# A decoder trunk's attention heads: last products, output copy and split emitted later, inside the next head's turn

## The chip, the cores and the metric

The kernel runs on one core of a Trainium2 chip. The metric is the device time in microseconds of one execution; lower is better. Times given are medians of several executions.

## The reference

The program is a decoder trunk of two layers on one sequence of 512 tokens and 1024 features, in float32: a gated linear attention layer with its convolutional feed-forward part, then keys and values computed once from the residual stream, then a sparse attention layer (NSA) with a second feed-forward part, and a final normalisation. The change touches the sparse attention alone. Cut to that:

```python
p_cmp = masked_softmax(q @ k_cmp * scale, cmp_end <= pos)     # compressed branch, 31 blocks
o_cmp = p_cmp @ v_cmp
p_sel = masked_softmax(rope(q) @ k_sel * scale, kpos <= qpos) # selected blocks
o_sel = p_sel @ v_sel
p_win = masked_softmax(rope(q) @ k_win * scale, win_mask)     # sliding window of 512
o_win = p_win @ v_win
o = gates[0] * o_cmp + gates[1] * o_sel + gates[2] * o_win
x = x + o @ w_o
```

There are 16 heads of 64 features in 4 groups that share keys and values. With 512 tokens, 8 blocks of 64 and up to 16 selected, all blocks are selected and the window covers all of the past, so both branches are causal attention over the whole sequence, each with its own keys and values.

## The kernel before, in words

Activations lie feature by token (`xT`, eight tiles of 128 x 512). To keep float32 accuracy, every large product is made of three passes of a reduced format: each operand is split into a rounded part `h` (ScalarE, ACT) and a remainder `l` (VectorE, DVE, or GpSimd, POOL), and `mm3` (L235 to L239) multiplies hh, lh and hl on TensorE (PE).

The attention stage is `nsa_att`. For one head, two generators emit its instructions piece by piece:

- `scores(h)` (L866) makes the softmax of a head in six score groups over the four blocks `i` of 128 queries and the two branches `b`. A group multiplies queries and keys (L882, L883), adds the causal mask by a product with an identity (L884), takes the row maximum on DVE (L886), and the exponential on ACT with the row sum beside it (L893). The result goes to `p_t`, one of ten buffers; the score bank `sc` has three. After half the groups a reciprocal (L902) and the gates (L903) give the scale of each row, and the rows are scaled by DVE (L913), by ACT (L909) or in pieces of 128 columns by POOL (L911, in `pool_parts`, L151), as the string `SCALE_ENGINE` says: POOL has block 0 of branch 0 and block 3 of branch 1.
- `values(h)` (L921) transposes the probabilities in five packs (L939, bank `tp`, two buffers), copies a pack to SBUF on ACT (L941, `pt_h`), subtracts on DVE (L943, `pt_l`), and two packs later multiplies by the values (`products`, L931, bank `po`, one buffer). The last two packs' products follow after the fifth pack (L948, L949), then two products for the compressed branch (L952). The output is evacuated by an ACT copy of its lower half (`lo`, L957) and a DVE addition (`o_t`, L958); after every second head `o_t` is split (L960).

The heads' loop (L984) interleaves the scores of head h+1 with the values of head h by the string `INTERLEAVE`:

```python
INTERLEAVE = "ssvsvsvsvs"
```

After it comes the rest of `values(h)` (L996), then the rest of the scores. Once in four heads the compressed branch of the next group runs: `compressed` (L836) makes its scores (L842, bank `pC`) and softmax, whose subtraction of the maximum is on POOL (L849) and whose exponential on ACT (L850); `compressed_t` (L858) transposes it. Between heads the loop emits `queries(f)` (rotary embedding by `rope`, L677, in POOL pieces `rot` and `sw`, then the split `q_s`) and, at a lower priority, a `query()` (a projection `pl` of 24 products, whose weights `w_raw` are copied by ACT, L159, and split by POOL, `w_l`) or a part of the output projection.

The code's order sets priorities only. A scheduler in the framework takes, engine by engine, the ready instruction of the highest priority and fixes the program's order; on the chip each engine then works through its own list in order and waits on semaphores.

Of the kernel before, what the change touches and what calls it, by code (L numbers as in the profile page):

```python
# [79 lines left out]
def tile_kernel(ctx: ExitStack, tc: tile.TileContext, a, out):  # L80
# [20 lines left out]
    def T(shape, dt, name):  # L101
        tag = TAGS.get(name, name)
        pool, n = home[tag]
        return pool.tile(shape, dt, name=name, tag=tag, bufs=n)

    def P(name):
        return T([128, 512], F32, name)
# [59 lines left out]
    def split(src, name, eng=DVE):  # L167
        h = T([128, S], F32R, name + "_h")
        ACT.activation(h, src, AF.Copy)  # L169
        l = T([128, S], F32R, name + "_l")  # L170
        eng.tensor_tensor(l, src, h, OP.subtract)  # L171
        return h, l
# [68 lines left out]
    def proj(src, xs, name, w=None, pool=False, m=128):  # L241
        n = len(xs)
        h, l = w or load_w(src, [128, n, m], pool=pool)
        ps = P(name)
        for k in range(n):
            mm3(ps[0:m], (h[:, k], l[:, k]), xs[k], k == 0, k == n - 1)
        return ps
# [407 lines left out]
    def nsa():  # L655
        with pools("nsa"):
            with pools("p_att"):
                os_ = nsa_att()
            with pools("p_proj"):
                for d in range(KT):  # L660
                    wo_part(os_, 4, d)

    def wo_part(os_, k0, d):
        add_x(d, proj(a["nsa_o"][d][:, k0:k0 + 4], os_[k0:k0 + 4], "pw", pool=k0 == 0))

    def nsa_att():
# [38 lines left out]
        def query():  # L705
            ps = proj(a["nsa_q"][len(Q)], xq, "pl" if len(Q) > 1 else "sc", pool=len(Q) > 1)
            q = T([128, S], F32, "qn")
            DVE.scalar_tensor_tensor(q, ps, 0.125, rb, OP.mult, OP.mult)
            Q.append(q)
# [3 lines left out]
        def queries(f):  # L713

            t = rope(Q[f])
            r = []
            for x in range(2):
                for hh in range(2):
                    n, o = slice(hh * 64, hh * 64 + 64), slice(64 - hh * 64, 128 - hh * 64)
                    y = T([128, S], F32R, "q_s")  # L720
                    if x == 0:
                        ACT.activation(y[n], t[n], AF.Copy)
                    else:
                        pool_parts(y[n], t[n], r[hh][n], OP.subtract)
                    nc.sync.dma_start(y[o].bitcast(F32), y[n].bitcast(F32))
                    r.append(y)
            for hh in range(2):
                QS[2 * f + hh] = (r[hh], r[2 + hh])
# [107 lines left out]
        def compressed(g):  # L836
            pC = P("pC")
            pCv = pC.rearrange("p (t c) -> p t c", t=4)
            for f in range(2):
                q = Q[2 * g + f]  # L840
                for i in range(4):
                    PE.matmul(pCv[:, i, f * 64:(f + 1) * 64], q[:, i * 128:(i + 1) * 128], BD[:, g],  # L842
                              start=True, stop=True)
            pc = CP[g] = T([128, 4, 4, 32], F32, "pcm")
            DVE.tensor_tensor(pc, pC.rearrange("p (t h n) -> p t h n", t=4, h=4),
                              cmask[:, :, None, :].to_broadcast([128, 4, 4, 32]), OP.add)
            mx = small([128, 4, 4], "mx", bufs=2)
            DVE.tensor_reduce(mx, pc, AX.X, OP.max)
            POOL.tensor_tensor(pc, pc, mx[:, :, :, None].to_broadcast([128, 4, 4, 32]), OP.subtract)  # L849
            ACT.activation(pc, pc, AF.Exp)  # L850
            sm = small([128, 4, 4], "smc", bufs=2)
            DVE.tensor_reduce(sm, pc, AX.X, OP.add)
            DVE.reciprocal(sm, sm)
            DVE.tensor_tensor(sm, sm, gate[:, :, 0, g * 4:g * 4 + 4], OP.mult)
            DVE.tensor_scalar(sm[:, 0], sm[:, 0], rowmask, None, OP.mult)
            POOL.tensor_tensor(pc, pc, sm[:, :, :, None].to_broadcast([128, 4, 4, 32]), OP.mult)

        def compressed_t(g):  # L858
            pT = P("pT")
            for i in range(4):  # L860
                PE.transpose(pT[:, i * 128:(i + 1) * 128], CP[g][:, i].rearrange("p a b -> p (a b)"), ident)
            CP[g] = split(pT, "pc")
# [58 lines left out]
        def values(h):  # L921
            g, gi = divmod(h, 4)
            pr = PR.pop(h)
            o_ps = P("po")
            todo = []

            def products():
                pack, th, tl = todo.pop(0)
                for b, j, c0 in pack:
                    for t in (th, tl):  # L930
                        PE.matmul(o_ps[:, j * 128:], V[b][:, j, g], t[:, c0:c0 + (4 - j) * 128],  # L931
                                  start=(b, j) == (0, 0) and t is th, stop=False)

            for pack in packs:
                tp = P("tp" if h < 15 or pack[0][1] % 2 else "sc")
                for b, j, c0 in pack:
                    for i in range(j, 4):
                        c = c0 + (i - j) * 128
                        PE.transpose(tp[:, c:c + 128], pr[i, b][:, j * 128:(j + 1) * 128], ident)  # L939
                th = T([128, S], F32R, "pt_h")  # L940
                ACT.activation(th, tp, AF.Copy)  # L941
                tl = T([128, S], F32R, "pt_l")
                DVE.tensor_tensor(tl, tp, th, OP.subtract)  # L943
                todo.append((pack, th, tl))
                if len(todo) > 2:
                    products()
                yield
            while todo:  # L948
                products()  # L949
            qd = slice(gi * 32, (gi + 1) * 32)  # L950
            for x in range(2):
                PE.matmul(o_ps, Vc[qd, g], CP[g][x][qd], start=False, stop=x == 1)  # L952
            hs = slice((gi % 2) * 64, (gi % 2) * 64 + 64)
            if gi % 2 == 0:
                half[0] = T([128, S], F32, "o_t")
            lo = T([128, S], F32, "lo")
            ACT.activation(lo[hs], o_ps[64:128], AF.Copy)  # L957
            DVE.tensor_tensor(half[0][hs], o_ps[0:64], lo[hs], OP.add)  # L958
            if gi % 2:
                os_.append(split(half[0], "o"))  # L960
            yield

        def run(g, n=99):
            for _ in range(n):
                if next(g, 1):
                    return
# [14 lines left out]
        queries(1)  # L981
        compressed(0)
        query()
        for h in range(16):  # L984
            gs = scores(h + 1) if h + 1 < 16 else None
            if h % 4 == 2 and h < 14:
                compressed(h // 4 + 1)
            gv = values(h)
            for n, c in enumerate(INTERLEAVE):
                if h == 0 and n == 6:  # L990
                    compressed_t(0)
                if c == "v":
                    run(gv, 1)
                elif gs:
                    run(gs, 1)
            run(gv)  # L996
            if gs:
                run(gs)
            if h % 4 == 3 and h < 14:
                compressed_t(h // 4 + 1)  # L1000
            if h % 2 == 1 and h // 2 + 2 < 8:
                queries(h // 2 + 2)
            if h in QUERY_HEAD:
                with tc.high_priority(offset=-50):
                    query()
            for d in range(KT):
                if WO_HEAD[d] == h:
                    with tc.high_priority(offset=-50):
                        wo_part(os_, 0, d)
# [102 lines left out]
```

## Time and profile before

| | us |
|---|---|
| median of 3 runs | 1331.68 |
| lowest and highest | 1331.22, 1332.91 |
| the profiled execution's own time | 1331.54 |
| span of its instructions | 1329.7 |
| busy: PE, DVE, ACT, POOL | 1312.2, 896.3, 610.8, 180.6 |

The span runs from the first instruction to the last; 1.8 us lie around it. Busy time is the time in which an engine had an instruction in work. Matmuls overlap, and their ends are modelled, so the time from one matmul's start to the next one's start tells more than busy time does. PE's granted clock is a share of 2.4 GHz. The attention heads run from about 730 to 935 us of the span.

### The profile page before, as it was taken

The page shows a single profiled execution, that of the slowest core. Times are in us where ns is not written, and L with a number is a line of the kernel's source. Part 1 is how long each engine was busy: PE and PEld are TensorE (multiplying, and loading weights), DVE is VectorE, ACT ScalarE, POOL GpSimd, SP SyncE. Part 2 cuts the span into 40 slices and gives each one's busy share as a digit, 9 for nine tenths or more (in the row PEclk, how much of TensorE's full clock was granted, in tenths as well). Part 3 has the DMA queues.
Part 4 walks back from the last instruction along what each step waited for, and adds up shares of the span by engine and source line. Part 5 has one row for each costly group of instructions (what it writes and reads, how often), then busy time and mean ns, then how long its engine had stood idle before and what let it go on. Part 6 is the DMA issues. An engine that isn't in the chain of part 4 may idle for free.

```text
span 1329.7 us, 17541 instructions
## 1 busy us (share of the span) xinstructions
PE 1312.2 (99%) x6498; PEld 1079.2 (81%) x6498; DVE 896.3 (67%) x1427; ACT 610.8 (46%) x1030; POOL 180.6 (14%) x454
## 2 busy tenths in 40 slices
PE   9999999999999999999999899999999999999998
PEld 6899988888888888888887677777888888888886
DVE  6888665577636763676765798888777736763672
ACT  6434544344314431443254687786554413441342
POOL 2000000000000000000236756653000000000000
PEclk9999999999999999999999899999999999999999
DMA  6122213333332333325543211211433332332331
GB/s 203 61 64 64 64 48 96 95 95 95 96 95 95 96 96 94 97 81 166 152 128 88 64 41 36 60 41 32 128 95 95 95 95 96 96 96 94 97 109 64
DMA packets 42246, 119.89 MB, mean 90 GB/s; under 512 B 5488, under 2 KB 8432, under 8 KB 42160
## 3 DMA queue, kind: packets, MB, share of 16 engines
q1 hardware_dynamic: 41152, 117.15, 29.0%
q10 hardware_dynamic: 1008, 1.61, 0.3%
q8 instruction: 51, 0.84, 0.3%
q14 instruction: 35, 0.29, 0.1%
HBM read 109.31 MB, written 2.10 MB: 84 GB/s over the span
## 4 chain that ended last, share of the span: by engine, by line
PE 90%; DVE 4%; POOL 1%; issue 1%; DMA 1%; ACT 1%; SPq 0%; POOLq 0%; ACTq 0%; DVEq 0%
PE pu L237 12%; PE pu L239 12%; PE pu L238 12%; PE pd L237 6%; PE pd L239 6%; PE pd L238 6%; PE po L931 3%; PE tp L939 3%; PE pw L237 2%; PE pw L239 2%; PE pw L238 2%; PE plv L550 2%; PE sc L882 2%; PE sc L883 1%; PE pv L237 1%
## 5 line engine op out<-in xcount | busy, mean ns | idle before, releaser
L159 ACT ACTIVATE w_h<-w_raw 128x1024 fp32r<-128x1024 f32 (+2 forms) x195 | 197.8, 1014 | 326.4 <-PE pd L239 129.9
L237 PE MATMUL pu<-x_h,w_h 128*128 128x512 f32 x704 | 274.1, 389 | 0.0
L238 PE MATMUL pu<-x_h,w_l 128*128 128x512 f32 x704 | 274.1, 389 | 0.0
L239 PE MATMUL pu<-x_l,w_h 128*128 128x512 f32 x704 | 273.9, 389 | 0.0
L164 DVE TENSOR_TENSOR w_l<-w_raw,w_h 128x1024 fp32r<-128x1024 f32 (+3 forms) x181 | 215.2, 1189 | 50.7 <-ACT w_h L159 48.6
L239 PEld LDWEIGHTS pu<-x_l,w_h 128*128 128x128 f32 x704 | 132.2, 188 | 27.6
L238 PEld LDWEIGHTS pu<-x_h,w_l 128*128 128x128 f32 x704 | 132.2, 188 | 27.3
L237 PEld LDWEIGHTS pu<-x_h,w_h 128*128 128x128 f32 x704 | 132.2, 188 | 27.3
L237 PE MATMUL pd<-m_h,w_h 128*128 128x512 f32 x304 | 120.2, 395 | 0.0
L239 PE MATMUL pd<-m_l,w_h 128*128 128x512 f32 x304 | 120.1, 395 | 0.0
L238 PE MATMUL pd<-m_h,w_l 128*128 128x512 f32 x304 | 120.0, 395 | 0.0
L286 DVE TENSOR_TENSOR u<-pu,rb 128x512 f32<-128x512 f32 x88 | 60.6, 689 | 81.2 <-PE pu L239 77.4
L264 DVE TENSOR_TENSOR xall<-xall,pd 128x512 f32<-128x512 f32 x40 | 27.5, 687 | 97.9 <-PE pd L239 97.8
L285 POOL MEMSET u<- 128x2 f32 x88 | 8.3, 99 | 620.9 <-DVE cv L291 602.5
L169 ACT ACTIVATE m_h<-cv 128x512 fp32r<-128x512 f32 x44 | 27.8, 632 | 115.2 <-DVE cv L294 115.2
L288 ACT ACTIVATE cv<-u,cols 128x512 f32<-128x512 f32 x88 | 71.1, 808 | 2.7 <-DVE u L286 1.9
L893 ACT ACTIVATE p_t<-sc,nm 128x128 f32<-128x128 f32 (+3 forms) x128 | 66.9, 529 | 8.6 <-DVE nm L886 7.8
L237 PEld LDWEIGHTS pd<-m_h,w_h 128*128 128x128 f32 x304 | 57.1, 188 | 14.1 <-ACT m_h L169 0.4
L239 PEld LDWEIGHTS pd<-m_l,w_h 128*128 128x128 f32 x304 | 57.1, 188 | 14.0 <-DVE m_l L171 0.2
L291 DVE SCALAR_TENSOR_TENSOR cv<-u,cols,cv 128x512 f32<-128x512 f32 x88 | 66.2, 752 | 3.0
L290 DVE SCALAR_TENSOR_TENSOR cv<-u,cols,cv 128x512 f32<-128x512 f32 x88 | 65.7, 746 | 3.7 <-ACT cv L288 3.4
L238 PEld LDWEIGHTS pd<-m_h,w_l 128*128 128x128 f32 x304 | 57.1, 188 | 13.7
(294 smaller groups left out, 2628.0 us busy)
## 6 DMA issues: line engine op xcount, KB each, us to landing
w_raw<-in_ffn_up_dram SPq DMA_DIRECT2D x88, 512.0 KB, 3.5
w_raw<-in_ffn_down_dram SPq DMA_DIRECT2D x32, 512.0 KB, 3.5
w_raw<-in_gla_v_dram SPq DMA_DIRECT2D x8, 512.0 KB, 3.6
w_raw<-in_gla_r_dram SPq DMA_DIRECT2D x8, 512.0 KB, 3.5
w_raw<-in_gla_o_dram SPq DMA_DIRECT2D x8, 512.0 KB, 3.6
w_raw<-in_kv_f_dram SPq DMA_DIRECT2D x8, 512.0 KB, 3.5
w_raw<-in_nsa_q_dram SPq DMA_DIRECT2D x8, 512.0 KB, 3.6
q_s<-q_s SPq DMA_DIRECT2D x32, 128.0 KB, 2.2
```

Of the source, the lines that this page charges most:

```text
L159: ACT.activation(h, raw, AF.Copy)
L164: DVE.tensor_tensor(l, raw, h, OP.subtract)
L237: MM.append(PE.matmul(ps, wh, xh, start=first, stop=False).ins)
L238: PE.matmul(ps, wl, xh, start=False, stop=False)
L239: PE.matmul(ps, wh, xl, start=False, stop=last)
L286: DVE.tensor_tensor(u[:, 2:], ps, rb[0], OP.mult)
L288: ACT.activation(c, u[:, 2:2 + S], AF.Identity, scale=col(w, 3 * jj + 2), bias=col(f"conv_b{layer}", jj))
L290: DVE.scalar_tensor_tensor(c, u[:, 1:1 + S], col(w, 3 * jj + 1), c, OP.mult, OP.add)
L291: DVE.scalar_tensor_tensor(c, u[:, 0:S], col(w, 3 * jj), c, OP.mult, OP.add)
L893: ACT.activation(pr[i, b], scv[:, bi], AF.Exp, bias=nm[:, i, b:b + 1], accum_out=su[:, i, b:b + 1])
L931: PE.matmul(o_ps[:, j * 128:], V[b][:, j, g], t[:, c0:c0 + (4 - j) * 128], start=(b, j) == (0, 0) and t is th, stop=False)
L939: PE.transpose(tp[:, c:c + 128], pr[i, b][:, j * 128:(j + 1) * 128], ident)
```

## The change

`values(h)` now yields once more after the compressed products, so that a head's end has two pieces: the last products (packs four and five and the compressed branch), and the output copy, addition and split. The loop no longer runs them at the end of head h's turn. It keeps the generator as `ending` and runs the first piece in the next head's turn after the first two score groups, and the second after that head's first transposed pack and one more score group. Heads 3, 7, 11 and 15 (`h % 4 == 3`) still end in their own turn. Lines behind the new `yield` have numbers one higher: `lo` is L958, `o_t` is L959.

```diff
--- before.py
+++ after.py
@@ -950,6 +950,7 @@
             qd = slice(gi * 32, (gi + 1) * 32)
             for x in range(2):
                 PE.matmul(o_ps, Vc[qd, g], CP[g][x][qd], start=False, stop=x == 1)
+            yield
             hs = slice((gi % 2) * 64, (gi % 2) * 64 + 64)
             if gi % 2 == 0:
                 half[0] = T([128, S], F32, "o_t")
@@ -981,6 +982,7 @@
         queries(1)
         compressed(0)
         query()
+        ending = None
         for h in range(16):
             gs = scores(h + 1) if h + 1 < 16 else None
             if h % 4 == 2 and h < 14:
@@ -993,9 +995,14 @@
                     run(gv, 1)
                 elif gs:
                     run(gs, 1)
-            run(gv)
+                if ending and n in (1, 3):
+                    run(ending, 1)
+            run(gv, 1)
             if gs:
                 run(gs)
+            if h % 4 == 3:
+                run(gv)
+            ending = gv
             if h % 4 == 3 and h < 14:
                 compressed_t(h // 4 + 1)
             if h % 2 == 1 and h // 2 + 2 < 8:
```

What the scheduler makes of it is shown at three places. In the names, `V_5089` and `V_5090` are the values of the two branches, `K_5085` and `K_5086` the keys of the first and second group of heads, `pl` a query's projection.

PE, end of head 1 (the difference; - is before, + is now):

```order
 L931 MATMUL po<-pt_l,V_5089 128x128
+L842 MATMUL pC<-BD,qn 128x64 x8
+L882 MATMUL sc<-K_5085,q_s 128x256
+L883 MATMUL sc<-K_5085,q_s 128x256
+L884 LDWEIGHTS identb
+L884 MATMUL sc<-negb,identb 128x256
+L882 MATMUL sc<-K_5085,q_s 128x512
+L883 MATMUL sc<-K_5085,q_s 128x512
+L884 LDWEIGHTS identb
+L884 MATMUL sc<-negb,identb 128x2x128
 L931 MATMUL po<-pt_h,V_5090 128x384
 L931 MATMUL po<-pt_l,V_5090 128x384
```

The scores of the compressed branch and two score groups stood behind the compressed products of this head; they now stand ahead of its last eight products (of which two are shown).

POOL, the same turn (the difference):

```order
 L151 TENSOR_TENSOR q_s<-rot,q_s 64x128 x8
-L151 TENSOR_TENSOR p_t<-p_t,su 128x128 x4
 L151 TENSOR_TENSOR rot<-qn,cosT 128x128 x3
 L151 TENSOR_TENSOR w_l<-w_raw,w_h 128x128 x8
 L151 TENSOR_TENSOR rot<-qn,cosT 128x128
+L151 TENSOR_TENSOR p_t<-p_t,su 128x128 x4
 L849 TENSOR_TENSOR pcm<-pcm,mx 128x512
```

The four pieces that scale block 3 of the head's scores stood ahead of three rotary pieces, the eight pieces of the weights' split and one more rotary piece; they now stand behind them, directly ahead of the compressed branch's subtraction. At heads 3, 5, 7 and 9 the same four pieces go behind rotary and weight pieces in the same way; at heads 7 and 9 the split has four pieces.

ACT, around the output copy of head 1, before:

```order
L957 ACTIVATE lo<-po 64x512
L169 ACTIVATE o_h<-o_t 128x512
L941 ACTIVATE pt_h<-tp 128x512
L893 ACTIVATE p_t,su<-sc,nm 128x128 x2
L941 ACTIVATE pt_h<-tp 128x512
L850 ACTIVATE pcm<-pcm 128x512
L893 ACTIVATE p_t,su<-sc,nm 128x256 x2
L941 ACTIVATE pt_h<-tp 128x512
```

and now:

```order
L893 ACTIVATE p_t,su<-sc,nm 128x128 x2
L958 ACTIVATE lo<-po 64x512
L850 ACTIVATE pcm<-pcm 128x512
L893 ACTIVATE p_t,su<-sc,nm 128x256 x2
L941 ACTIVATE pt_h<-tp 128x512
L169 ACTIVATE o_h<-o_t 128x512
L893 ACTIVATE p_t,su<-sc,nm 128x512
L941 ACTIVATE pt_h<-tp 128x512 x3
```

The exponential of the compressed branch (L850) and the two exponentials of 256 columns stood behind the copies of the next head's first two packs; they now stand ahead of both, with L850 right behind the output copy.

## Rows read from the trace of the kernel before

**Rows 1.** The page, part 1: busy us, share of the span, instructions.

```profile
PE 1312.2 (99%) x6498; PEld 1079.2 (81%) x6498; DVE 896.3 (67%) x1427; ACT 610.8 (46%) x1030; POOL 180.6 (14%) x454
```

**Rows 2.** Table of stretches: PE, PEld, DVE, ACT, POOL busy, PE clock, DMA share, GB/s.

```profile
734.00:735.60 1.60, 0.06 (x1) 0.00 (x0) 1.37 (x3) 1.60 (x6) 1.52 (x5) 1.00 0.34 76
735.60:742.40 6.80, 5.78 (x21) 4.66 (x22) 3.43 (x8) 2.58 (x7) 6.80 (x16) 0.50 0.47 116
...
760.00:940.00 180.00, 179.82 (x1044) 137.80 (x1044) 155.27 (x331) 135.53 (x345) 93.08 (x210) 1.00 0.16 42
```

**Rows 3.** PE's timeline behind head 1: start us, us, engine, line, out<-in.

```profile
764.44 0.39 PE L237 MATMUL pl<-x_h,w_h 128*128 128x512 f32 x1
764.77 0.50 PE L882 MATMUL sc<-K,q_s 128*128 128x512 f32 x1
765.11 0.40 PE L883 MATMUL sc<-K,q_s 128*128 128x512 f32 x1
...
768.07 0.39 PE L239 MATMUL pl<-x_l,w_h 128*128 128x512 f32 x1
768.30 0.39 PE L237 MATMUL pl<-x_h,w_h 128*128 128x512 f32 x1
```

**Rows 4.** Chain of waits, heads 1 and 2: start us, us, engine, tile, line, count.

```profile
758.21 1.16 PE po L931 x9
...
760.03 1.93 PE pC L842 x16
...
762.95 0.44 PE tp L939 x4
...
772.09 1.39 PE po L931 x8
```

**Rows 5.** Timelines of ACT, then DVE, last pack of head 3.

```profile
783.01 0.59 ACT L941 ACTIVATE pt_h<-tp 128x512 fp32r<-128x512 f32 x1
...
784.33 1.04 ACT L159 ACTIVATE w_h<-w_raw 128x1024 fp32r<-128x1024 f32 x1
...
784.03 0.68 DVE L943 TENSOR_TENSOR pt_l<-tp,pt_h 128x512 fp32r<-128x512 f32 x1
```

**Rows 6.** POOL's timeline around head 5; in brackets idle time and its releaser.

```profile
806.90 1.73 POOL L151 TENSOR_TENSOR p_t<-p_t,su 128x128 f32<-128x128 f32 x4 [0.72 <-DVE su L903]
808.93 1.28 POOL L151 TENSOR_TENSOR rot<-qn,cosT 128x128 f32<-128x128 f32 x3 [0.30 <-DVE qn L708]
810.17 3.81 POOL L151 TENSOR_TENSOR w_l<-w_raw,w_h 128x128 fp32r<-128x128 f32 x8
...
814.37 1.04 POOL L849 TENSOR_TENSOR pcm<-pcm,mx 128x512 f32<-128x512 f32 x1
```

**Rows 7.** PE's timeline: score groups after head 1, end of a query in head 5.

```profile
761.77 0.36 PE L882 MATMUL sc<-K,q_s 128*128 128x256 f32 x1
...
762.79 0.60 PE L939 MATMUL tp<-kc,p_t 128*128 128x128 f32 x4
...
763.76 0.61 PE L939 MATMUL tp<-kc,p_t 128*128 128x128 f32 x4
...
807.59 0.44 PE L239 MATMUL pl<-x_l,w_h 128*128 128x512 f32 x1
```

**Rows 8.** ACT's timeline behind head 1.

```profile
760.07 0.59 ACT L957 ACTIVATE lo<-po 64x512 f32<-64x512 f32 x1 [0.75 <-PE po L952]
...
765.66 0.63 ACT L850 ACTIVATE pcm<-pcm 128x512 f32<-128x512 f32 x1 [0.45 <-POOL pcm L849]
...
767.10 0.60 ACT L941 ACTIVATE pt_h<-tp 128x512 fp32r<-128x512 f32 x1
```

**Rows 9.** Timelines of DVE, then PE: output of head 3, first product of head 4.

```profile
786.71 0.68 DVE L958 TENSOR_TENSOR o_t<-po,lo 64x512 f32<-64x512 f32 x1 [1.05 <-ACT lo L957]
...
788.76 0.47 PE L931 MATMUL po<-pt_h,V 128*128 128x512 f32 x1
```

## The prediction, made before the changed kernel had run

> **What bounds the kernel now.** I read the page first: TensorE (PE) is busy 99% of the span [rows 1]. Ends of matmuls are modelled, so this share alone proves little, and the table of stretches comes next. From 760 to 940 us, where the attention heads run, PE is busy 179.8 of 180 us at a granted clock of 1.00, VectorE (DVE) 155.3 and ScalarE (ACT) 135.5 [rows 2]. So PE sets the pace there, and a change is worth what it gives or takes on PE.
>
> What PE still loses is read in the timeline, from start to start. A 512-column product takes 0.23 us (768.07 to 768.30); at 764.44 it takes 0.33 us and the next one, at 764.77, 0.34 us [rows 3]: a score group that waits a little for a score buffer. In the chain of waits, nine last products of head 1 take 1.16 us, but eight of head 2 take 1.39 us [rows 4]: they wait for the split of the last pack. Such short waits are all that the change can win; the reader should see how small they are beside the 25 us that DVE, the next busiest engine, has left in 180.
>
> **The change, part by part.** No instruction is added or removed, so PE's work is unchanged (0, bounds 0.3 us either way, for other neighbours of the same products). It moves three things.
>
> (a) The last products behind two score groups. At heads 1, 5 and 9 the score groups now stand ahead of the last eight products, and ACT and DVE have the 1.0 us of these to empty score buffers. The two waits of [rows 3], 0.1 us each, go, and I allow as much again for the groups behind: 0.4 us at heads 1 and 5, 0.2 us at head 9. At heads 2 and 6 the last pack's split is covered: 1.39 us less 8/9 of 1.16 us, 0.35 us each [rows 4]. Gain 1.7 us, bounds 0.5 to 3. At head 0 PE's order does not change, and at heads 3, 7 and 11 the code does not delay the products at all.
>
> (b) A weight copy ahead of the last pack's copy. At head 3 ACT now copies the query's weights (1.04 us) before it copies the last pack, not after; behind it come that copy, 0.59 us, and DVE's subtraction, 0.68 us [rows 5]. The weights' copy starts as the query's products end, so the split is done about 2.4 us later; the products that read it are due 1.9 us after the query by my count of the order. Cost 0.5 us at head 3, and 0.1 us at head 7, where the weights are half as long. Sum 0.6, bounds 0 to 1.5.
>
> (c) The queue of GpSimd (POOL), and with it ACT's. This is the large term. POOL works in order. At heads 1, 3 and 5 the four pieces of a score's scaling (1.73 us) stood before the rotary pieces and the split of the query's weights; now they stand behind them. At heads 1 and 5 the compressed branch's subtraction (L849) stands behind all of this, and its exponential on ACT (L850) is now right behind the head's output copy, ahead of the exponentials of the second score group and of the copy of the next head's first pack.
>
> The sum, with time 0 at the start of the query's last product at head 5, 807.59 [rows 7]. POOL's rotary pieces wait for the query and start at 808.93, +1.34. Three of them 1.28, eight pieces of the split 3.81, one more rotary piece 0.43 (a third of 1.28) end at +6.9; four pieces of scaling, 1.73, end at +8.6; the subtraction, 1.04, ends at **+9.6** [rows 6]. PE does in the meantime: that last product 0.2, the rest of a score group 0.3, four transpositions 0.44, four products 0.5, the compressed scores 1.93, two score groups 1.02 (761.77 to 762.79), eight products 1.03 (8/9 of 1.16) and one of the two compressed products, 0.33 [rows 4, 7]. The head's last product starts at about **+5.7**. POOL thus delivers 3.9 us after that start. ACT has made the output copy by then: in [rows 8] it runs from 760.07 for 0.59 us, and at 0.33 us a product the last one began at 759.7, so ACT is through 1.0 us after it. It stands still until 3.9. The exponential and the two exponentials of 256 columns take 1.44 us (765.66 to 767.10) and free the second score group's buffer at 5.3. PE wants this buffer for its third group from there: 0.33 for the last product, twice 0.97 for a transposed pack and a group of 512 columns (762.79 to 763.76) and one product of 0.3 [rows 3, 7] make it due at **2.6**. PE waits 2.7 us; the first pack's copy, 0.6 us behind the exponentials, holds the product behind that group for another 0.1, and I add 0.2 for hand-overs. **3.0 us at head 1, 3.0 us at head 5.** Before, the same exponential stood behind the copies of the first two packs and waited 0.45 us on POOL [rows 8], at no cost to PE.
>
> Bounds of each: below, 0, if PE has more work of its own in between than I count; above, 4.5, if the backlog that ACT and DVE have after it holds PE again. I take 3.0, as every duration in it has its row. At head 9 the split has four pieces, about 1.9 us less, and nearly all is hidden: 0.3 us (0 to 1.2). At head 3 no compressed branch is in the queue; the transposition that reads the first piece of scaling is due 6.5 to 6.9 us after the query, and that piece is done at 6.9 + 0.43: 0.5 us (0 to 2).
>
> Sum: -1.7 + 0.6 + 3.0 + 3.0 + 0.3 + 0.5 = **+5.7 us** on the profiled execution's own 1331.54 us, 1337.2. That execution lies 0.14 us under the median of the three runs, 1331.68, so the change is 5.5 us against the median: **1337.2 us**. For scale, 0.2% is 2.7 us, about what a measurement of this kernel can tell from no change.
>
> (d) The output copy itself. The output has a single bank, so the next head's first product waits for copy and addition. At head 3 the addition ends at 787.38 and that product starts at 788.76, 1.4 us later [rows 9]; the new order keeps as much work of PE between them, so where ACT is free this costs nothing (0 to 0.3 us a head). The Trainium skill, page "Perfetto Trace Analysis", section "Optimizing Tensor Performance", wants independent groups of matmuls to rotate through banks, so that the evacuation of one lies under the next one's matmuls; by it a later evacuation of a single bank is a loss. The 1.4 us of slack in the trace say otherwise here, and I follow the trace.
>
> **Rivals.** Each is a mechanism with its place.
>
> No change: ACT's hold at heads 1 and 5 is hidden. For it: the term hangs on 2.6 against 5.3 us, counted by hand, and POOL's spans are rough. Against it: POOL's order is fixed, and its pieces are regular. It decides at a POOL chain shorter by 2.7 us. Then 1331.54 - 1.7 + 0.6 + 0.8 = 1331.2. That the scheduler undoes the change belongs here; the orders shown above speak against it. Chance 0.22.
>
> Faster: the hold is hidden, and the short waits go at twelve or thirteen heads, 0.35 us each as in [rows 4]: 1331.54 - 4.4 = 1327.1. Against it: heads 0, 3, 7 and 11 keep their order. Chance 0.09.
>
> Slower, with PE at half clock. After PE did 0.06 us of work in 1.6 us (734.0 to 735.6) its granted clock stood at 0.50, that is 1.2 of 2.4 GHz, for 6.8 us [rows 2]. A hold of 3 us could bring that back at both places. A stretch at half clock costs at most half its length, 3.4 us: 1337.2 + 6.8 = 1344.0. Against it: PE stood longer before that stretch than these holds would make it. The Trainium skill, "TensorE: Matmul & The Clock Gate", section "HAM oscillation", tells of kernels whose waits between bursts of matmuls send the clock to half every time; the one such stretch here agrees with it. Chance 0.13.
>
> **How the numbers follow.** Forecast 0.56, no change 0.22, faster 0.09, half clock 0.13. The forecast's own bounds, 1.5 to 4.5 us a hold with the other terms, reach from 1333 to 1341; with most of the no-change case below and a good part of the clock case above, the range is 1330.6 to 1342.5. Slower by over 0.2%: 0.56 + 0.13 = 0.69; within: 0.22; faster: 0.09.
>
> **What would show it.** Right: after the output copies of heads 1 and 5 ACT idles some 3 us before L850, released by POOL's subtraction; PE's third score group behind them is late by as much; the wait at the end of head 2 is gone. Wrong in (c): PE starts there without a gap over 0.3 us. Wrong in (b): no wait in head 3's last products. Wrong as a whole: a time under 1334.3 us, or a gap at a place not named here, at the first product of a head above all.

## The result and the profile after

| | before | after |
|---|---|---|
| median of the runs compared, us | 1331.45 (4 runs) | 1354.98 (4 runs) |
| lowest and highest | 1330.1 to 1332.91 | 1354.26 to 1357.21 |
| profiled execution's own time, span | 1331.54, 1329.7 | 1355.65, 1353.9 |

The change makes the kernel slower by the ratio 1.0179 (95% interval 1.0163 to 1.0195): 23.5 us, where +5.5 was forecast and 1342.5 us was the top of the range. The direction was right and the size was wrong by a factor of four.

The page's first line:

```profile
PE 1319.1 (97%) x6498; PEld 1085.2 (80%) x6498; DVE 896.5 (66%) x1427; ACT 611.5 (45%) x1030; POOL 179.4 (13%) x454
```

The attention heads in the table of stretches (columns as in [rows 2]):

```profile
760.00:940.00 180.00, 164.09 (x918) 125.96 (x918) 138.15 (x300) 121.15 (x313) 91.02 (x205) 0.94 0.16 42
```

Against [rows 1] every engine has as many instructions as before, in a longer span. Against the third line of [rows 2] PE now works 164.1 of 180 us, not 179.8, at a mean clock of 0.94, not 1.00. So two things were lost: PE waits, and after most of its longer waits it works at half clock. The view of PE's waits over 745 to 965 us (us in all, times, longest) says for whom it waits. Before the change that view has no row there.

```profile
PE tp L939 <- POOL p_t L151: 8.1, 4, 3.0
PE sc L882 <- ACT p_t L893: 4.7, 3, 2.6
PE tp L939 <- DVE pt_l L943: 2.0, 1, 2.0
PE po L931 <- DVE pt_l L943: 1.4, 3, 0.8
PE po L931 <- DVE o_t L959: 0.6, 1, 0.6
```

That is 16.8 us. The half clock is read from four stretches of the table (us, PE's busy time, clock, DMA share, GB/s); the fifth row is a stretch with a wait and no fall:

```profile
769.50:776.30 6.80, 5.85 (x18) 0.50 0.00 0
800.30:803.60 3.30, 3.30 (x12) 0.50 0.04 13
827.60:834.40 6.80, 5.00 (x14) 0.50 0.11 39
889.00:892.40 3.40, 3.17 (x10) 0.50 0.12 42
853.00:860.00 7.00, 5.46 (x36) 1.00 0.35 94
```

PE is busy for 17.3 us of the four, and half of that, 8.7 us, is lost. Waits and half clock make 25.5 us, against 24.2 between the two spans. Two stretches at half clock ahead of this window also differ: that of head 0 costs 1.7 us, where it cost 2.9 before, and one at 656.8 us costs 1.7, which the kernel before does not have and the undelayed ninth run below has too. What makes up the rest is open.

**How one place comes about.** Behind head 1, first PE, then POOL, then ACT of the changed kernel:

```profile
756.93 0.33 PE L882 MATMUL sc<-K,q_s 128*128 128x384 f32 x1
...
757.51 0.40 PE L239 MATMUL pl<-x_l,w_h 128*128 128x512 f32 x1
...
766.66 0.33 PE L939 MATMUL tp<-kc,p_t 128*128 128x128 f32 x1 [1.76 <-POOL p_t L151]
...
770.45 0.69 PE L882 MATMUL sc<-K,q_s 128*128 128x384 f32 x1 [2.63 <-ACT p_t L893]
```

```profile
757.40 3.49 POOL L151 TENSOR_TENSOR q_s<-rot,q_s 64x128 fp32r<-64x128 f32 x8 [5.08 <-issue]
760.97 1.31 POOL L151 TENSOR_TENSOR rot<-qn,cosT 128x128 f32<-128x128 f32 x3
762.24 3.59 POOL L151 TENSOR_TENSOR w_l<-w_raw,w_h 128x128 fp32r<-128x128 f32 x8
765.80 0.45 POOL L151 TENSOR_TENSOR rot<-qn,cosT 128x128 f32<-128x128 f32 x1
766.22 1.47 POOL L151 TENSOR_TENSOR p_t<-p_t,su 128x128 f32<-128x128 f32 x4
767.65 1.04 POOL L849 TENSOR_TENSOR pcm<-pcm,mx 128x512 f32<-128x512 f32 x1
```

```profile
768.72 0.63 ACT L850 ACTIVATE pcm<-pcm 128x512 f32<-128x512 f32 x1 [4.65 <-POOL pcm L849]
```

The same of the kernel before, PE and POOL:

```profile
753.41 0.34 PE L882 MATMUL sc<-K,q_s 128*128 128x384 f32 x1
...
757.76 0.45 PE L239 MATMUL pl<-x_l,w_h 128*128 128x512 f32 x1
...
753.88 3.63 POOL L151 TENSOR_TENSOR q_s<-rot,q_s 64x128 fp32r<-64x128 f32 x8 [2.33 <-ACT pt_h L941]
757.59 1.59 POOL L151 TENSOR_TENSOR p_t<-p_t,su 128x128 f32<-128x128 f32 x4
```

Read it from the top. L882 at 756.93 opens the head's last score group, L239 at 757.51 is the query's last product. Before, the group came 4.35 us ahead of that product; now it comes 0.58 us ahead. POOL's split of the queries (`q_s`) starts 0.47 us after the start of that L882, in both kernels: by the code it writes one of six buffers, whose old content the last score group still reads. The view names other releasers there (ACT `pt_h`, or only "issue"), but the distance returns, 0.42 to 0.47 us in eleven of the twelve kernels of this study. In the twelfth, the ninth run, it is 0.68 us: there ACT's half of the split ended last, at 747.90, and POOL started at 747.97. So POOL's queue starts 3.5 us later, and behind it stand the rotary pieces, the weights' split, the scaling and L849, in the order that was shown ahead of the prediction. The scaling's first piece ends at 766.6; the transposition that reads it has waited 1.76 us. L849 ends at 768.7; ACT has stood still for 4.65 us, and the third score group gets its buffer 2.63 us late. Then PE's clock is at 0.50 from 769.5 to 776.3.

### The profile page after: what moved, and what is told of

The parts are those of the page before. It is cut to its first block, busy times and chain, and to the rows that moved or that the text cites. A ratio compares the mean times of both kernels' runs of the same rounds, so it can differ in the third digit from the quotient of the medians.

```text
span 1353.9 us, 17541 instructions
## 1 busy us (share of the span) xinstructions
PE 1319.1 (97%) x6498; PEld 1085.2 (80%) x6498; DVE 896.5 (66%) x1427; ACT 611.5 (45%) x1030; POOL 179.4 (13%) x454
## 4 chain that ended last, share of the span: by engine, by line
PE 86%; DVE 4%; POOL 4%; issue 2%; ACT 2%; DMA 1%; SPq 0%; POOLq 0%; ACTq 0%; DVEq 0%
PE pu L237 12%; PE pu L239 12%; PE pu L238 12%; PE pd L237 6%; PE pd L239 6%; PE pd L238 6%; PE po L931 2%; PE pw L237 2%; PE pw L239 2%; PE pw L238 2%; PE tp L939 2%; PE plv L550 2%; POOL q_s L151 1%; POOL w_l L151 1%; PE sc L882 1%
## 5 line engine op out<-in xcount | busy, mean ns | idle before, releaser
L239 PE MATMUL pu<-x_l,w_h 128*128 128x512 f32 x704 | 273.9, 389 | 0.0
L239 PEld LDWEIGHTS pu<-x_l,w_h 128*128 128x128 f32 x704 | 132.2, 188 | 27.6
L239 PE MATMUL pd<-m_l,w_h 128*128 128x512 f32 x304 | 120.1, 395 | 0.0
L239 PEld LDWEIGHTS pd<-m_l,w_h 128*128 128x128 f32 x304 | 57.1, 188 | 14.0 <-DVE m_l L171 0.2
```

Source lines behind the costliest of these rows:

```text
L239: PE.matmul(ps, wh, xl, start=False, stop=last)
```

## The experiments

Ratios are against the kernel before, measured beside each kernel on the same chip. Each edit lets the scheduler fix the order anew, so that a run can change more than the operation it names. Two theories stood from the start: (A) the delay of the last products puts the last score group, and with it POOL's queue, late; (B) the late output copy of the single bank does it.

**1 and 2. One half of the change each.**

```diff
-                if ending and n in (1, 3):
-                    run(ending, 1)
-            run(gv, 1)
+                if ending and n == 3:
+                    run(ending)
+            run(gv, 2)
```

> Only the output copy, addition and split of a head are delayed, to behind the next head's first transposed pack; the last products stay in the head's own turn. Theory A (delaying the last products puts a head's last score group and with it POOL's queue late; the copy is harmless): 1332 us, within 3 us of the kernel before, and no wait of PE over 1 us from head 1 on. Theory B (the late evacuation of the single output bank is the cause): at least half of the change's loss of 23 us remains, 1343 us or more, with waits at a head's first product.

Measured: 1335.22 us, 1.0024 (1.0015 to 1.0033). The waits over the heads are 1.7 us in all, none above 0.5:

```profile
PE po L931 <- DVE pt_l L943: 0.8, 2, 0.5
PE sc L882 <- ACT p_t L893: 0.5, 2, 0.3
PE pw L237 <- DVE xall L264: 0.4, 1, 0.4
```

The other half, the products delayed as in the change and the copy directly behind them:

```diff
-                if ending and n in (1, 3):
-                    run(ending, 1)
+                if ending and n == 1:
+                    run(ending)
```

> The last products are delayed behind two score groups as in the change, but copy, addition and split follow them at once, two steps earlier than in the change. Theory A: all of the loss stays, 1355 us, within 4 us, with waits of PE's fourth transposition on POOL (1.8, 3.0, 1.8 and 1.5 us in the changed kernel) at the same places. Theory B: the loss shrinks to below half, under 1343 us.

Measured: 1357.21 us, 1.0187 (1.0172 to 1.0202), with the waits of the change:

```profile
PE tp L939 <- POOL p_t L151: 7.5, 4, 2.9
PE sc L882 <- ACT p_t L893: 5.5, 3, 2.6
```

So the products carry the loss. The late copy by itself costs 0.2%, about 3 us, and no wait for the output's bank is in its view; theory B falls.

**3 and 4. POOL's part.** The compressed subtraction on DVE, and in another kernel the split of the query weights on DVE:

```diff
-            POOL.tensor_tensor(pc, pc, mx[:, :, :, None].to_broadcast([128, 4, 4, 32]), OP.subtract)
+            DVE.tensor_tensor(pc, pc, mx[:, :, :, None].to_broadcast([128, 4, 4, 32]), OP.subtract)
```

> The changed kernel with the compressed branch's subtraction of the maximum (L849) on DVE, so that its exponential no longer stands behind POOL's queue. Theory A: the score-buffer waits behind it (2.6 us at head 1's end, 1.8 us at head 5's) go, and the half clock that follows them there (about 2.9 and 2.1 us by the rows) goes or shrinks; the transposition waits on POOL (1.8, 3.0, 1.8, 1.5 us) stay: 1346 us, 1344 to 1350. Theory C (one backlog of POOL, which costs PE the same wherever it comes out): the transposition waits grow by what the others lose, 1352 us or more.

Measured: 1346.87 us, 1.0114 (1.0097 to 1.0131). The score-buffer waits are gone, the waits for the scaling stand as they were:

```profile
PE tp L939 <- POOL p_t L151: 8.6, 4, 2.8
```

Half clock still costs 1.7 us behind head 1 and 1.5 behind head 3; behind head 5 there is none. So from head 1 on the two kinds of wait add up and do not stand in for each other: theory C falls. In head 0 the edit costs something: PE's wait for L856 grows to 5.9 us, from 2.6 and one of 1.1 just before it.

```diff
-            ps = proj(a["nsa_q"][len(Q)], xq, "pl" if len(Q) > 1 else "sc", pool=len(Q) > 1)
+            ps = proj(a["nsa_q"][len(Q)], xq, "pl" if len(Q) > 1 else "sc", pool=False)
```

> The changed kernel with the split of the query weights (w_l, eight pieces, 3.6 to 3.8 us a query) on DVE in place of POOL. Theory A with POOL's queue as the bottleneck: up to 3.8 us less at the ends of heads 1, 3 and 5 (4.7, 3.2 and 4.2 us of waits there) with most of the half clock behind them (2.9, 1.6, 2.1 us): 1338 us, 1335 to 1342. Theory D (the score group that comes late on PE sets all of it, since the scaling needs its row sums, and POOL's work behind it is no matter): 1348 us or more.

Measured: 1338.79 us, 1.0049 (1.0034 to 1.0064), by the ratios some 17 us less than the change. At the end of head 1 the last score group is still nearly as late as in the change (L882 0.57 us ahead of the query's last product), yet ACT's stop before L850 is 1.63 us, not 4.65:

```profile
764.23 0.63 ACT L850 ACTIVATE pcm<-pcm 128x512 f32<-128x512 f32 x1 [1.63 <-POOL pcm L849]
```

So a late group alone costs little (theory D falls): it is the late start with 3.6 us of weights behind it. Of what remains, 6.5 us by the ratio, 2.4 are such waits through L850, and some 4.6 lie behind head 9. There POOL splits weights of the output projection, which this edit leaves on POOL: waits of 2.9 us and 3.4 us at half clock stand there as in the change.

**5 and 6. Both on DVE, and a control.** The fifth kernel has both edits, the sixth the last one alone in the kernel before.

> The changed kernel with both the split of the query weights and the compressed subtraction on DVE. Theory A (POOL's queue): the two score-buffer waits of 1.4 us that were left behind L850 go too, the wait of 3.5 us and its half clock at head 10 stay: 1335 us, 1333 to 1338. Theory E (DVE, which gets all of this work, becomes the next bound): 1339 us or more, with waits of PE on pt_l.

Measured: 1332.48 us, 1.0003 (0.9993 to 1.0012). The kernel is back at the time of before, with the products still delayed and the late order of PE still in place; no wait of PE over the heads exceeds 0.8 us. Not all of that is the loss undone: this run has no half clock in head 0, where the kernel before loses 2.9 us (last section), and PE's short waits over the heads still make 2.6 us, where before has none. So of the 23.5 us some 20 are shown to be gone in its profiled execution; for the rest runs 9 and 10 are the cleaner pair. Better than expected: I had left the place behind head 9 standing, but its wait came through L850 too.

> The kernel before, with the split of the query weights on DVE in place of POOL: the control for the last runs. Theory A (before the change POOL's queue is hidden, and DVE has room): no change, 1332 us, within 2.5. Theory E (the weights' split costs DVE time that PE feels): 1336 us or more, so that what was left of the loss with the weights on DVE isn't the delay's.

Measured: 1330.97 us, 0.9992 (0.9983 to 1.0002). In the kernel before, the same relief of POOL can't be told from no change: there POOL's queue was hidden. Theory E falls in both runs.

**7 and 8. The late group.**

```diff
-INTERLEAVE = "ssvsvsvsvs"
+INTERLEAVE = "ssvssvsvsv"
```

> The changed kernel with INTERLEAVE = ssvssvsvsv: the score groups come one pack earlier, and the scheduler then puts the last group of a head ahead of some ten of the query's products, where the change has two of them behind it. Theory A (the last score group is late, and POOL's queue with it): PE's waits for POOL's scaling fall from 8.1 us to under 3 and the half clock at head 4 goes; the hold of L850 gets shorter but stays: 1342 us, 1337 to 1347. Theory F (the order inside POOL's queue alone, weights ahead of the subtraction, makes the loss, whenever it starts): 1350 us or more.

Measured: 1343.52 us, 1.0083 (1.0068 to 1.0098). At the end of head 1 the last L882 starts at 754.70, 3.0 us ahead of the query's last product, not 0.58, and POOL follows at once:

```profile
755.12 3.74 POOL L151 TENSOR_TENSOR q_s<-rot,q_s 64x128 fp32r<-64x128 f32 x8 [3.79 <-PE sc L882]
758.94 1.48 POOL L151 TENSOR_TENSOR p_t<-p_t,su 128x128 f32<-128x128 f32 x4
760.37 1.71 POOL L151 TENSOR_TENSOR rot<-qn,cosT 128x128 f32<-128x128 f32 x4
762.03 3.38 POOL L151 TENSOR_TENSOR w_l<-w_raw,w_h 128x128 fp32r<-128x128 f32 x8
765.37 1.05 POOL L849 TENSOR_TENSOR pcm<-pcm,mx 128x512 f32<-128x512 f32 x1
```

Here the view names the releaser of the queries' split itself: PE's L882. The scaling is back ahead of the weights, and PE's waits for it are gone (8.1 to 0 us); L849 still stands behind the weights; it ends 8.7 us after the start of the query's last product, not 11.2, and the waits through L850 remain (4.0 us in two, with half clock behind both). Theory F's time, 1350 us or more, did not come. But the run does not part the queue's start from its order, since the earlier group also brought the scaling ahead of the weights. Where the order stayed, with L849 behind the weights, the waits through L850 only went from 4.7 to 4.0 us.

> The kernel before with INTERLEAVE = ssvssvsvsv: the control for the earlier last group. Theory A: no change within 4 us, 1332; the order of the groups is worth something only where the last group is late. If it is worth as much here as in the changed kernel (7 us or more less), the late group is not the change's doing.

Measured: 1334.09 us, 1.0011 (1.0002 to 1.0021), no gain in the kernel before. So what the earlier group gives back in the changed kernel, by the ratios some 12 us, belongs to the change.

**9 and 10. All three on DVE, with and without the delay.** The edits of runs 3 and 4, and L856 in the same way:

```diff
-            POOL.tensor_tensor(pc, pc, sm[:, :, :, None].to_broadcast([128, 4, 4, 32]), OP.mult)
+            DVE.tensor_tensor(pc, pc, sm[:, :, :, None].to_broadcast([128, 4, 4, 32]), OP.mult)
```

> The kernel before with the split of the query weights and both operations of the compressed branch (L849, L856) on DVE, so that neither a score's scaling nor the compressed branch stands behind another's work on POOL. By the rows of before PE waits 2.7 us on the compressed product (L856) in head 0 and then works 6.8 us at half clock: 5 us less, 1327 us, 1324 to 1329. If DVE is as late as POOL there: 1331 us or more.

Measured: 1329.0 us, 0.9973 (0.9962 to 0.9983): faster than both kernels, by 3.6 us against before, where 5 were expected. From 728 to 746 us PE is busy 17.48 of 18 us at full clock, where the kernel before has 14.38 at 0.81:

```profile
728.00:746.00 18.00, 17.48 (x104) 13.18 (x103) 17.95 (x41) 14.35 (x40) 12.56 (x25) 1.00 0.28 74
```

The profiled execution took 1326.88 us, 2.1 less than the median, so that its rows may flatter the run.

> The changed kernel with the same three on DVE; against the run before it, it shows what the delay is worth where POOL is out of its way. The prediction's term (a), short waits that go, 1.7 us: 1 to 3 us under that run, 1325 us. Theory G (the short waits only move, the delay is worth nothing): within 1.5 us of it. Theory H (the delay costs by itself, by the late last group): 2 us or more above it.

Measured: 1329.62 us, 0.998 (0.9971 to 0.9989), 0.6 us above the ninth, and the intervals overlap. Theory G holds: where POOL is out of the way, delaying the ends of the heads neither gains nor costs anything that these times show. A small cost isn't excluded: PE's waits from 720 to 965 us make 3.9 us here and 1.5 in the ninth run. The two largest entries here, the second of them for the output's bank:

```profile
PE pw L237 <- DVE xall L264: 1.4, 1, 1.4
PE po L931 <- DVE o_t L959: 1.2, 2, 0.6
```

## Why the prediction was wrong in size

**What bounds the kernel: right.** PE set the pace, and the loss came from what makes PE wait.

**(a) The gain of 1.7 us: not there.** The wait at the end of head 2 is gone: its last eight products take 1.04 us (1.39 in [rows 4]). But the tenth run has other waits that the ninth does not have, and the time did not fall, as the two runs show (+0.6, not -1.7).

```profile
780.46 1.04 PE po L931 x8
```

**(b) The weight copy ahead of the last pack's copy: about right.** 0.5 and 0.1 us were forecast at heads 3 and 7; the waits of the last products for `pt_l` are 0.3 and 0.2 us there.

**(c) The hold through POOL: the right mechanism, each place mis-sized.** By the rows of PE's waits and of the half clock:

| behind head | forecast, us | waits of PE | half clock |
|---|---|---|---|
| 1 | 3.0 | 1.8 + 2.6 | 2.9 |
| 3 | 0.5 | 3.0 | 1.7 |
| 5 | 3.0 | 1.8 + 1.8 | 2.5 |
| 7 | not priced | 1.5 | 0 |
| 9 | 0.3 | 2.0 + 0.6 + 0.3 | 1.6 |

The column of forecasts makes 6.8 us, the waits 15.4 and the half clock 8.7. The forecast was short by 18 us; 8.6 of these are waits that were sized too small or not priced, and 8.7 are the clock.

Three steps failed.

The first is "POOL's rotary pieces wait for the query and start at 808.93, +1.34". In the changed order they wait for the split of the queries ahead of them, and that waits for the last score group, which the scheduler now puts only 0.58 us ahead of the query's last product. Behind head 1 they started 3.46 us after that product, 2.1 us later than forecast, and L849 ended at +11.2, not +9.6. At head 3 this step makes all of the wait's miss: PE was due at +6.9, as forecast, but the scaled piece let it go at +9.9, not +7.3. The new place of that group could be read from the order, and the buffer on which POOL waits for it could be followed in the code; I took the start from a row of the kernel before, where another wait ended last.

The second is that at heads 1 and 5 only the second reader of POOL's queue was priced. The fourth transposition of the first pack reads the scaled block, and stands ahead of the third score group; I counted that wait at head 3 alone (0.5 us, it took 3.0). PE waits twice: the second wait came out at 2.63 us where 2.7 were worked out, and the first added 1.76. That the second agrees is luck: L849 ended 1.6 us later than forecast, and the first wait made PE late by about as much. ACT's stop, "some 3 us", was 4.65 behind heads 1 and 5 alike. The third run shows that these waits are separate. At head 7 the scaling's move was seen, and not priced at all; the 1.5 us there are a gap for which the prediction named no cause.

The third is the chance of half clock. It stood as a rival with 0.13 and 3.4 us a place, because PE had "stood longer" before the fall that the trace showed. With the first two steps mended, PE stands 4.4 us in two pieces behind head 1, and the fall costs 2.9 us there and 8.7 us in all. The Trainium skill, "TensorE: Matmul & The Clock Gate", section "HAM oscillation", had said that waits (there on DMA) between bursts of matmuls take the clock down; the four stretches above agree with it, the fifth, with 1.5 us of waiting at full clock, does not.

**(d) The output copy: nearly right.** Nothing was forecast, 0 to 0.3 us a head; the first run gives 3 us for the twelve heads that it delays, 0.3 us each if it is all the copy's. Its rows do not say so: its waits over the heads make 1.7 us, none for the bank, and it has the half clock of 1.7 us ahead of the heads that the ninth run has too. In the change one wait for the bank shows, 0.6 us behind head 9.

The upper bound of each hold was 4.5 us. The waits themselves stayed inside it, 4.4 us behind head 1 and 3.6 behind head 5, though for another reason than the backlog it was taken from. What broke it was the half clock, 2.9 and 2.5 us there, which stood apart as a rival, and the range's top took in only a part of that rival.

## What to carry to other kernels

When a piece is emitted later in a program whose order a scheduler fixes, look first at where the scheduler puts the work that another engine's queue waits for, and count buffer releases among these waits: here a product on PE that read a buffer last set the start of 11 us of work on POOL. Then price every instruction that reads from such a queue, not only the last one. And relieve a queue where the bottleneck waits for it. In the kernel before, moving the weights' split alone off POOL gave nothing that shows; together with the two operations of the compressed branch it was worth 0.27%, and the rows show that gain in head 0, where PE had waited for L856. The delay added nothing to that.

## What the runs showed of the hardware

Whether the clock falls did not follow from one wait's length here. In the kernel before, PE stood in head 0, waiting for L856 (2.6 us, and 1.1 us for a score buffer just before it), and then had 6.8 us at half clock [rows 2]; in the fifth run it waited 3.0 us at the same place, with 0.5 before it, and the clock stayed at 1.00 through the stretch. First the view of before, then the fifth run's:

```profile
PE pT L861 <- POOL pcm L856: 2.6, 1, 2.6
PE sc L882 <- ACT p_t L893: 1.1, 1, 1.1
...
PE pT L861 <- POOL pcm L856: 3.0, 1, 3.0
```

```profile
733.00:740.00 7.00, 3.55 (x22) 1.00 0.30 69
740.00:747.00 7.00, 7.00 (x49) 1.00 0.18 30
```

Nor does it always fall while PE stands: behind head 1 it fell at 769.5, with PE's next product at 770.45, but behind head 3 at 800.3, a microsecond after the work had begun again at 799.26. And in the changed kernel the same two waits in head 0, 1.1 and 2.6 us, were followed by 3.4 us at half clock, not 6.8. So the cost of a wait of 1.5 to 3 us has more than one value, and a sum should carry them as a span. What else decides between them is left open.

Left open too is why the scheduler puts the last score group later once the products are delayed; that it does is read from its order, and the seventh run shows what an earlier place gives back. More buffers for the split queries, which might take the wait for that group away, were not tried.
